# The norm of x taken behind PSUM, value columns first, and the first nine entries in written order

## The chip, the cores and the metric

The kernel runs on one NeuronCore of one Trainium2 chip. The metric is device time in microseconds (us) of one launch, a median over runs; lower is better. The clock of TensorE (PE in the rows) has two levels, 1.2 and 2.4 GHz. VectorE is DVE, ScalarE is ACT, GpSimd is POOL, and SyncE (SP) issues the DMAs.

## The reference

Two transformer blocks run on one sequence of 256 tokens with 1024 features. Only the beginning matters here: the root-mean-square norm of x and the projection of the first block.

```python
def rmsnorm(x, g):
    xf = x.astype(jnp.float32)
    y = xf * lax.rsqrt(jnp.mean(xf * xf, axis=-1, keepdims=True) + EPS)
    return (y * g.astype(jnp.float32)).astype(x.dtype)
...
        hn = rmsnorm(h, norm_mix_g[l])
        proj = hn @ w_in[l]
        fq, fk, fv, ff, gq, gf, gi, gg = jnp.split(proj, split_idx, axis=-1)
```

fq, fk, fv and the forget logits ff (8 columns) feed a causal attention, gq, gf, gi and gg a gated linear recurrence (HGRN). Everything is float32. The norm of a token is one factor per row of x, so it may be applied before the projection or to its result.

## The kernel before, in words

Every large product is made of three float32r matmuls: each operand is split into a high part, rounded to float32r, and the low rest, and `mm3` (L205 to L208) multiplies high by high, low by high, high by low. Weights come from HBM as granules of 1 MB (`Granule`, `feed`, three raw buffers `w`), one DMA each on SP's queue, issued as soon as a raw buffer is free. A granule is used in two halves. Each half is split by `split_next`: ACT casts it (tile `wh`, L142), DVE subtracts (tile `wl`, L143), into one of six pairs of split buffers.

The program is a list of entries (`prog`). An entry is one half of a granule, a unit of 24 matmuls of 256 columns or 12 of 512, with the pieces of other work that are hung behind it. `emit` walks the list: it writes the unit, then calls `pump`, which splits one further half, then the evacuation of PSUM (`evac`), then the pieces. In the kernel before `start` splits both halves of the first granule before any unit, so a unit's own half is always two calls of `pump` behind it. TensorE's order is the written one. For the other engines a scheduler sets the order from its own estimate of times; only `start` runs under a manual schedule (L737).

`start` loads the gain and x (L631, L633) and the first granule, warms TensorE with 12 matmuls of the identity (L642), squares x, takes the row factor with a power on POOL (L297), scales x (L651, L653), turns it with 16 transposes (L669) and splits the turned x into `xh` and `xl` (L328, L329). The gain is applied in that split.

Then come the projections of block one, in this order: gf (4 units, sigmoid), gq (4, silu), gg (4, silu), fv with ff (4), fq and fk (8), gi (4), and the keys of the memory attention (8). Hung behind them are `vectors` (turns small vectors, L693), `forget` (two activations with different tables, L930 and L931, and a scan), the nine levels of the recurrence, `m_load` and two `m_s` (load and norm of the memory rows: squares at L304, scaling at L315) and `load_later` with `difference` (four loads of lambda, L719, and a few instructions on `lamv`, L725 to L729, which only block two needs). PSUM tiles `mm` have two buffers, so the third unit pair needs the first one's evacuation.

Of the kernel before, what the change touches and what calls it, by code (L numbers as in the profile page):

```python
# [39 lines left out]
def two_blocks(ctx: ExitStack, tc: tile.TileContext, a: dict, out: bass.AP):  # L40
# [48 lines left out]
    def s_t():  # L89
        return psum.tile([P, 512], F32, tag="s", name=nm("s"), bufs=4)  # L90
# [26 lines left out]
    def feed():  # L117
        while at_dma[0] < len(stream) and at_split[0] >= 2 * (at_dma[0] - N_RAW + 1):
            g = stream[at_dma[0]]
            g.raw = wraw.tile([P, g.nk, g.ncol], F32, tag="w", name=nm("w"))  # L120
            src = g.src.rearrange("(k p) c -> p k c", p=P)
            if at_dma[0]:
                nc.sync.dma_start(g.raw, src)
            else:
                for c in (slice(0, P), slice(P, 2 * P)):
                    nc.sync.dma_start(g.raw[:, :, c], src[:, :, c])
            at_dma[0] += 1

    def split_next(pieces=None, low=V):
        g, i = stream[at_split[0] // 2], at_split[0] % 2  # L130
        if g.by_col:
            c = g.ncol // 2
            src, shape = g.raw[:, :, i * c:(i + 1) * c], [P, g.nk, c]
        else:
            k = g.nk // 2
            src, shape = g.raw[:, i * k:(i + 1) * k, :], [P, k, g.ncol]
        hi = wspl.tile(shape, F32R, tag="wh", name=nm("wh"))
        lo = wspl.tile(shape, F32R, tag="wl", name=nm("wl"))
        g.parts[i] = (hi, lo)
        at_split[0] += 1  # L140
        if pieces is None:
            S.copy(hi, src)  # L142
            low.tensor_tensor(lo, src, hi.bitcast(F32), op=ALU.subtract)  # L143
        else:
            k = g.nk // 2
            for p in (np.s_[:, 0:k, :], np.s_[:, k:, :]):
                def piece(p=p):
                    S.copy(hi[p], src[p])
                    G.tensor_tensor(lo[p], src[p], hi[p].bitcast(F32), op=ALU.subtract)
# [31 lines left out]
    def emit():  # L181

        for fn, pieces in prog:
            evac = fn() if fn is not None else None
            todo = later[:]
            later.clear()
            for f in todo:
                f()
            if fn is not None:
                pump()  # L190
            if evac is not None:
                evac()
            for f in pieces:
                f()
# [10 lines left out]
    def mm3(o, lh, ll, rh, rl, first, last):  # L205
        PE.matmul(o, lh, rh, start=first, stop=False)  # L206
        PE.matmul(o, lh, rl, start=False, stop=False)  # L207
        PE.matmul(o, ll, rh, start=False, stop=last)  # L208
# [109 lines left out]
    def xn_half(t):  # L318
        return R[4][:, t * D:(t + 1) * D]
# [306 lines left out]
    w_in = a["w_in"][0]  # L626

    def start():
        xin = a["x"][0].rearrange("(t p) d -> p t d", p=P)
        grow = R[5][0:8, 0:P]  # L630
        nc.sync.dma_start(grow, a["norm_mix_g"][0].rearrange("(k p) -> k p", p=P))  # L631
        for t in range(2):
            nc.sync.dma_start(h[:, t, :], xin[:, t, :])  # L633
        feed()
        V.memset(half, -0.5)
        V.memset(one, 1.0)
# [8 lines left out]
        o = [x.rearrange("p (k t) -> p k t", k=2) for x in (s_t(), s_t(), s_t(), s_t(), tp_t(), tp_t())]  # L645
        o = [o[k][:, 0, :] for k in range(6)] + [o[k][:, 1, :] for k in (2, 3)]

        def scale(t, n, r):
            x = xn_half(t)[:, HALVES[n]]
            if n > t:  # L650
                S.mul(x, h[:, t, HALVES[n]], r[:, 0:1])  # L651
            else:
                V.tensor_scalar(x, h[:, t, HALVES[n]], r[:, 0:1], None, op0=ALU.mult)  # L653

        ss = [sm_t(), sm_t()]
        for n in range(2):
            square(h[:, 0, HALVES[n]], ss[0][:, n:n + 1], (S, V)[n])
        r0 = rstd_row(ss[0])
        scale(0, 0, r0)
        for n in range(2):  # L660
            square(h[:, 1, HALVES[n]], ss[1][:, n:n + 1], (S, V)[n])
        scale(0, 1, r0)
        r1 = rstd_row(ss[1])
        for n in range(2):
            scale(1, n, r1)
        V.tensor_copy(g, go)
        for t in range(2):
            for k in range(8):
                PE.transpose(o[k][:, t * P:(t + 1) * P], xn_half(t)[:, k * P:(k + 1) * P], ident)  # L669
# [41 lines left out]

        def load_tables():
# [174 lines left out]
    def fv_units():  # L887
        gs_ = [Granule(w_in[kq * 512:(kq + 1) * 512, 1024:1544], 4, 520, False) for kq in range(2)]
        st = {}

        def unit(i):
            if i == 0:
                st["o"] = [(mm_t(), tp_t()) for _ in range(2)]
            w = part(gs_[i // 2], i % 2)
            for t in range(2):
                tok = slice(t * P, (t + 1) * P)
                for k in range(2):
                    for c in range(2):
                        cs = slice(c * 260, (c + 1) * 260)
                        mm3(st["o"][t][c][:, 0:260], r32(xh[:, 2 * i + k, tok]), r32(xl[:, 2 * i + k, tok]),  # L900
                            w[0][:, k, cs], w[1][:, k, cs], i == 0 and k == 0, i == 3 and k == 1)
            release()

            def ev():
                for t in range(2):
                    copy = V.tensor_copy if t else S.copy
                    o = st["o"][t]
                    ff.append(sm_t())
                    copy(fv[:, t, 0:260], o[0][:, 0:260])
                    copy(ff[t], o[1][:, 252:260])  # L910
                    copy(fv[:, t, 260:512], o[1][:, 0:252])
            return ev if i == 3 else None

        return [(lambda i=i: unit(i), gs_[i // 2] if i % 2 == 0 else None) for i in range(4)]
# [113 lines left out]
    u_ = []  # L1028
    for g in range(2):
        u_ += a_units(cols(w_in, 2056, g), XT, ev_gf(g))  # L1030
    for g in range(2):
        u_ += a_units(cols(w_in, 1544, g), XT, ev_silu(q_[:, g * 512:(g + 1) * 512]))
    u_ += b_units(w_in[:, 3080:3592], XT, lambda t, o: ev_silu(gs[:, t * 512:(t + 1) * 512])(0, o))
    u_ += fv_units()
    for g in range(2):
        u_ += a_units(cols(w_in, 0, g), XT, ev_to(R[2][:, g * 512:(g + 1) * 512], 0.125))
        u_ += a_units(cols(w_in, 512, g), XT, ev_to(R[2][:, 1024 + g * 512:1024 + (g + 1) * 512]))
    u_ += rows(w_in, 2568, 1, gi) + grid(xkw, 0, 4, R[5], None, ME)
    fox = Heads(fox_scores, fox_turn, fox_pv)
    run(u_, {  # L1040
        1: [lambda: start.vectors()], 2: [lambda: start.load_tables()], 6: [lambda: start.tables()],
        7: [lambda: start.load_later()], 9: [levels[0]], 11: [levels[1]],
        12: [m_load, levels[2], lambda: start.difference()], 13: [levels[3]], 14: [levels[4]], 15: [forget],
        16: [levels[5], m_s0], 17: [levels[6]], 18: [levels[7], m_s1, load_bias(0)], 19: [levels[8]],
        20: [load_bias(1, 2, 3)], 21: [fox.S(0)], 23: [fox.T(0), fox.S(1)], 25: [fox.V(0), m_t0],
        26: [fox.S(2), m_t1], 27: [fox.T(1)], 28: [fox.S(3), h_out(0)], 29: [fox.V(1), h_out(1)],
        30: [fox.T(2)], 31: [h_turn(0)], 32: [fox.V(2), fox.T(3)], 33: [h_turn(1)], 34: [fox.V(3)],
    })
# [338 lines left out]
    emit()  # L1387
# [49 lines left out]
```

## Time and profile before

| | |
|---|---|
| Median of 3 runs | 915.65 us (915.59 to 916.92) |
| The profiled execution's own time | 914.16 us |
| Its span, first to last instruction | 912.3 us |
| PE busy | 898.0 us (98%) |
| DVE busy | 588.4 us (64%) |
| ACT busy | 488.8 us (54%) |
| POOL busy | 130.0 us (14%) |
| HBM read | 160.34 MB, 177 GB/s over the span |

A timeline row reads: start and duration in us from the span's start, engine, source line, operation, out<-in tiles, partitions x elements, count, and in brackets the idle time before it with what ended it. Rows of equal instructions that follow each other are merged. PE's busy time counts overlapping matmuls, so the distance between the starts of two matmuls is the pace.

### The profile page before, as it was taken

Reading aid. Unit: us, or ns where it says so; the run is one execution under the profiler, and the core shown is the slowest. Engines: PE = TensorE matmul, PEld = TensorE weight load, DVE = VectorE, ACT = ScalarE, POOL = GpSimd, SP = SyncE. Lnnn points to the kernel's source line nnn. Section 1 sums busy time; section 2 is a strip of 40 time slices with the busy share of each in tenths; the row PEclk is TensorE's granted clock in tenths of the full one; section 3 lists DMA queues with packets and bytes.
Section 4 is the critical chain, followed back from the end, with each engine's and each line's share of the span. In section 5 each row is a group of like instructions: output and inputs, shape, how many; then the busy total and the mean of one; then the engine's idle time right before and its main releaser. Section 6 shows DMA issues by size and latency. Waiting matters only on the chain.

```text
span 912.3 us, 15217 instructions
## 1 busy us (share of the span) xinstructions
PE 898.0 (98%) x6213; PEld 823.9 (90%) x6213; DVE 588.4 (64%) x858; ACT 488.8 (54%) x743; POOL 130.0 (14%) x141
## 2 busy tenths in 40 slices
PE   8999999999999999999999999999999999999997
PEld 7999898898899999999898899999998789999995
DVE  5778775755575444555776455776756777766664
ACT  6745753555455444444654545667443676555552
POOL 3102220000002111111104000221211201101101
PEclk9999999999999999999999999999999999999999
DMA  8776544543555555555374555434555455555531
GB/s 271 256 253 186 185 155 164 198 153 114 167 193 192 195 190 193 189 185 185 131 250 135 183 179 185 139 131 133 200 185 185 161 185 183 188 201 193 166 135 47
DMA packets 117972, 162.39 MB, mean 178 GB/s; under 512 B 3647, under 2 KB 90509, under 8 KB 117901
## 3 DMA queue, kind: packets, MB, share of 16 engines
q1 hardware_dynamic: 117901, 161.41, 53.4%
q8 instruction: 49, 0.80, 0.3%
q14 instruction: 22, 0.18, 0.1%
HBM read 160.34 MB, written 1.06 MB: 177 GB/s over the span
## 4 chain that ended last, share of the span: by engine, by line
PE 90%; DVE 4%; ACT 2%; DMA 2%; POOL 1%; issue 1%; SPq 0%; DVEq 0%; POOLq 0%; ACTq 0%
PE mm L206 19%; PE mm L207 19%; PE mm L208 19%; PE s L208 8%; PE s L206 8%; PE s L207 8%; DMA w<-in_w_in_dram 2%; PE s L792 1%; POOL sm L297 1%; DVE wl L143 1%; PE tp L1068 1%; PE s L1060 1%; PE tp L337 1%; ACT wh L142 1%; PE s L1212 1%
## 5 line engine op out<-in xcount | busy, mean ns | idle before, releaser
L143 DVE TENSOR_TENSOR wl<-w,wh 128x1024 fp32r<-128x1024 f32 (+1 forms) x283 | 355.4, 1261 | 182.4 <-ACT wh L142 180.8
L142 ACT CAST wh<-w 128x1024 fp32r<-128x1024 f32 (+1 forms) x284 | 296.1, 1048 | 306.0 <-PE mm L207 190.2
L206 PE MATMUL mm<-xh,wh 128*128 128x256 f32 x1120 | 317.8, 284 | 0.0
L207 PE MATMUL mm<-xl,wh 128*128 128x256 f32 x1120 | 313.9, 280 | 0.3
L208 PE MATMUL mm<-xh,wl 128*128 128x256 f32 x1120 | 313.3, 280 | 0.0
L206 PEld LDWEIGHTS mm<-xh,wh 128*128 128x128 f32 x1120 | 211.3, 189 | 3.9 <-issue 2.3
L207 PEld LDWEIGHTS mm<-xl,wh 128*128 128x128 f32 x1120 | 211.2, 189 | 2.0 <-DVE xl L329 0.7
L208 PEld LDWEIGHTS mm<-xh,wl 128*128 128x128 f32 x1120 | 211.3, 189 | 0.0
L206 PE MATMUL s<-wh,mh 128*128 128x512 f32 x176 | 69.8, 396 | 0.0
L207 PE MATMUL s<-wl,mh 128*128 128x512 f32 x176 | 69.0, 392 | 0.0
L208 PE MATMUL s<-wh,ml 128*128 128x512 f32 x168 | 66.1, 393 | 0.0
L297 POOL TENSOR_TENSOR sm<-sm,half 128x1 f32<-128x1 f32 (+2 forms) x24 | 20.3, 847 | 234.2 <-DVE sm L310 221.7
L1103 POOL TENSOR_TENSOR r<-r 128x512 f32<-128x512 f32 x16 | 25.3, 1583 | 148.6 <-ACT r L1101 148.6
L206 PE MATMUL mm<-eh,wh 128*128 128x256 f32 x160 | 45.7, 286 | 0.0
L207 PE MATMUL mm<-el,wh 128*128 128x256 f32 x160 | 44.8, 280 | 0.0
L208 PE MATMUL mm<-eh,wl 128*128 128x256 f32 x160 | 44.7, 280 | 0.0
L208 PE MATMUL s<-wh,mh 128*128 128x512 f32 x112 | 44.1, 393 | 0.0
L1362 POOL TENSOR_TENSOR r<-r 128x512 f32<-128x512 f32 x11 | 21.4, 1946 | 148.0 <-DVE r L1350 124.2
L206 PE MATMUL s<-wh,ml 128*128 128x512 f32 x104 | 40.9, 394 | 0.0
L207 PE MATMUL s<-wl,ml 128*128 128x512 f32 x104 | 40.7, 392 | 0.0
L207 PEld LDWEIGHTS s<-wl,mh 128*128 128x128 f32 x176 | 33.1, 188 | 6.9
L206 PEld LDWEIGHTS s<-wh,mh 128*128 128x128 f32 x176 | 33.1, 188 | 6.7
(273 smaller groups left out, 1377.7 us busy)
## 6 DMA issues: line engine op xcount, KB each, us to landing
w<-in_w_in_dram SPq DMA_DIRECT2D x39, 1024.0 KB
w<-in_w_dram SPq DMA_DIRECT2D x32, 1024.0 KB
w<-in_w_up_dram SPq DMA_DIRECT2D x22, 1024.0 KB
w<-in_w_down_dram SPq DMA_DIRECT2D x11, 1024.0 KB
w<-in_w_xkv_dram SPq DMA_DIRECT2D x8, 1024.0 KB
w<-in_w_out_dram SPq DMA_DIRECT2D x8, 1024.0 KB
w<-in_w_xq_dram SPq DMA_DIRECT2D x4, 1024.0 KB
w<-in_w_xo_dram SPq DMA_DIRECT2D x4, 1024.0 KB
```

What stands on the lines that cost most here:

```text
L142: S.copy(hi, src)
L143: low.tensor_tensor(lo, src, hi.bitcast(F32), op=ALU.subtract)
L206: PE.matmul(o, lh, rh, start=first, stop=False)
L207: PE.matmul(o, lh, rl, start=False, stop=False)
L208: PE.matmul(o, ll, rh, start=False, stop=last)
L297: G.tensor_tensor(r[:, :n], v[:, :n], half.to_broadcast([P, n]), op=ALU.pow)
L337: PE.transpose(o[:, k * P:(k + 1) * P], xn[:, kk * P:(kk + 1) * P], ident)
L792: PE.matmul(o, k_[:, x], q2, start=True, stop=True)
L1060: PE.matmul(s[:, t, :], xq[:, j, t * P:(t + 1) * P], xkT[:, j, :], start=(c == 0), stop=(c == 1))
L1068: PE.matmul(o[:, c * T:(c + 1) * T], xv[:, m, cs], pt[:, m, :], start=(m == 0), stop=(m == 1))
L1103: G.tensor_tensor(tt, ra, ra, op=ALU.mult)
L1362: G.tensor_tensor(yv, yg, yv, op=ALU.mult)
```

## The change

- `start` turns x as it is, without its norm, in 16 transposes of h. The gain is still applied in the split of the turned x, now token half by token half. The row factors are made later (`factor`), kept as a column (`rt`) and, by one matmul (`row_factors`), as a row on all partitions (`rB`). They multiply each projection on its way out of PSUM: in `ev_gf` and `ev_token` on DVE ahead of the sigmoid or silu, elsewhere as the scale of the copy.
- The fv units come first, and x is split k by k as they need it.
- The first nine entries (`emit(9)`) get a chain of dependencies per engine, for ACT, DVE, POOL and SP, that keeps their instructions in written order (`in_order`). Instructions of later entries have no such chain. In these nine entries `pump` runs behind the evacuation instead of ahead of it.
- The pieces are hung at other entries, and the gain's load goes to ACT's queue.

```diff
     def do(*pieces):
         prog.append((None, list(pieces)))
 
+    @contextmanager
+    def in_order():
...
+            if i >= n and ins.engine in last:
+                tc.add_manual_dep(ins, last[ins.engine].name,
...
+    def emit(first=0):
...
+        for i, (fn, pieces) in enumerate(prog):
+            with (in_order() if i < first else nullcontext()):
+                evac = fn() if fn is not None else None
...
+                if fn is not None and i >= first:
+                    pump()
+                if evac is not None:
+                    evac()
+                if fn is not None and i < first:
+                    pump()
+                for f in pieces:
+                    f()
...
+    def split_x(i, t):
+        for k in (2 * i, 2 * i + 1):
+            split_to(XT, np.s_[:, k, t * P:(t + 1) * P], turned(t, k), start.g[:, k:k + 1])
+
+    def factor(t):
+        ss = sm_t()
+        for n in range(2):
+            square(h[:, t, HALVES[n]], ss[:, n:n + 1], (S, V)[n])
+        V.tensor_copy(rt[:, t:t + 1], rstd_row(ss)[:, 0:1])
...
-        for _ in range(12):
+        for _ in range(8):
             PE.matmul(o, ident, ident, start=True, stop=True)
...
+        pieces = []
+        for low in (V, G):
+            split_next(pieces, low)
+
+
         for t in range(2):
             for k in range(8):
-                PE.transpose(o[k][:, t * P:(t + 1) * P], xn_half(t)[:, k * P:(k + 1) * P], ident)
+                PE.transpose(turned(t, k), h[:, t, k * P:(k + 1) * P], ident)
+            split_x(0, t)
+            if t == 0:
+                for piece in pieces[0:2]:
+                    piece()
+            fv_part(0, t)
+        release()
+        split_x(1, 0)
+        pieces[2]()
+        split_x(1, 1)
+        pieces[3]()
...
     def ev_gf(g):
         def ev(i, o):
             s = slice(g * 512, (g + 1) * 512)
-            S.activation(f_[:, s], o, AF.Sigmoid)
+            V.tensor_tensor(f_[:, s].rearrange("p (b t) -> p b t", b=2), o.rearrange("p (b t) -> p b t", b=2), rB2,
+                            op=ALU.mult)
+            S.activation(f_[:, s], f_[:, s], AF.Sigmoid)
...
-    emit()
+    emit(9)
```

What the built program then holds, in three places.

DVE where the turned x is split (`s` are the turned tiles, `lamv` and `lam` the lambda vectors of `difference`, an entry beyond the ninth). Before, the lambda instructions stood in the third pair of granules:

```order
L143 TENSOR_TENSOR wl_563<-w_429,wh_562 128x1040
L725 TENSOR_TENSOR lamv<-lamv 128x128
L726 TENSOR_REDUCE lam<-lamv 128x2
L143 TENSOR_TENSOR wl_579<-w_429,wh_578 128x1040
L728 TENSOR_TENSOR lam<-lam 128x1
L729 TENSOR_SCALAR lam<-lam 128x1
L143 TENSOR_TENSOR wl_628<-w_492,wh_627 128x1040
```

Now:

```order
L352 SCALAR_TENSOR_TENSOR xl<-s_110,g_130,xh 128x128
L352 SCALAR_TENSOR_TENSOR xl<-s_111,g_130,xh 128x128
L770 TENSOR_TENSOR lamv<-lamv 128x128
L352 SCALAR_TENSOR_TENSOR xl<-s_110,g_130,xh 128x128
L352 SCALAR_TENSOR_TENSOR xl<-s_111,g_130,xh 128x128
L771 TENSOR_REDUCE lam<-lamv 128x2
L352 SCALAR_TENSOR_TENSOR xl<-s_108,g_130,xh 128x128
L352 SCALAR_TENSOR_TENSOR xl<-s_109,g_130,xh 128x128
L773 TENSOR_TENSOR lam<-lam 128x1
```

The lambda instructions moved into the split of x for the second unit.

ACT around the evacuations of gf and gq. Before (`r_87` is the sigmoid's and the silu's target, `mm` the PSUM tile):

```order
L142 CAST wh_252<-w_115 128x1024
L142 CAST wh_280<-w_115 128x1024
L142 CAST wh_331<-w_117 128x1024
L142 CAST wh_362<-w_117 128x1024
L753 ACT_TABLE_LOAD
L753 ACTIVATE r_87<-mm_227 128x512
L142 CAST wh_397<-w_200 128x1024
L142 CAST wh_425<-w_200 128x1024
```

Now (`wh_439` and `wh_484` are the two halves of the second gf granule, `wh_517` the first of gq, `P_446` the scratch of `forget`):

```order
L797 ACT_TABLE_LOAD
L797 ACTIVATE r_87<-r_87 128x512
L138 CAST wh_439<-w_147 128x1024
L988 ACT_TABLE_LOAD
L988 ACTIVATE P_446<-P_446 8x256
L989 ACT_TABLE_LOAD
L989 ACTIVATE P_446<-P_446,one 8x256
L138 CAST wh_484<-w_147 128x1024
L797 ACT_TABLE_LOAD
L797 ACTIVATE r_87<-r_87 128x512
L138 CAST wh_517<-w_319 128x1024
```

The cast of a half stands directly behind the evacuation of the unit that runs ahead of it, where before four casts stood ahead of the first sigmoid.

DVE at the first of these evacuations now (`r_92` holds the memory rows, `r_90` the row factors); before, the scaling of memory rows stood among the levels:

```order
L333 TENSOR_SCALAR sm_852<-sm_823 128x1
L338 SCALAR_TENSOR_TENSOR r_92<-r_92,sm_854,g_708 128x512
L795 TENSOR_TENSOR r_87<-mm_366,r_90 128x512
L338 SCALAR_TENSOR_TENSOR r_92<-r_92,sm_854,g_708 128x512
L333 TENSOR_SCALAR sm_949<-sm_920 128x1
L338 SCALAR_TENSOR_TENSOR r_92<-r_92,sm_951,g_708 128x512 x2
L139 TENSOR_TENSOR wl_440<-w_147,wh_439 128x1024
```

Three scalings of memory rows moved ahead of the low part `wl_440`, two of them with a power on POOL between.

## Rows read from the trace of the kernel before

**Rows 1.** The page's first part: busy time by engine.

```profile
PE 898.0 (98%) x6213; PEld 823.9 (90%) x6213; DVE 588.4 (64%) x858; ACT 488.8 (54%) x743; POOL 130.0 (14%) x141
```

**Rows 2.** Waits of PE, 0 to 160 us: total, times, longest, in us.

```profile
PE s L669 <- DVE r L653: 0.9, 1, 0.9
```

**Rows 3.** Timeline from the start, all engines.

```profile
1.34 5.49 PE L642 MATMUL mm<-ident 128*128 128x128 f32 x24 [1.34 <-POOL ident masks.py:199]
...
5.98 0.56 POOL L297 TENSOR_TENSOR sm<-sm,half 128x1 f32<-128x1 f32 x1 [4.69 <-DVE sm L310]
...
7.12 0.66 PE L669 MATMUL s<-ident,r 128*128 128x128 f32 x4
...
10.73 1.57 ACT L328 ACTIVATE xh<-s,g 128x256 fp32r<-128x256 f32 x4 [1.55 <-DVE g L666]
...
11.24 1.66 DVE L329 SCALAR_TENSOR_TENSOR xl<-s,g,xh 128x256 fp32r<-128x256 f32 x4 [0.60 <-ACT xh L328]
...
14.49 0.19 PEld L207 LDWEIGHTS mm<-xl,wh 128*128 128x128 f32 x1 [0.33 <-DVE xl L329]
```

**Rows 4.** Chain of waits, 33 to 42 us: start, length, what.

```profile
35.00 0.12 PE mm L206
35.12 0.13 PE mm L207
35.27 1.06 ACT wh L142
36.33 0.51 ACT r L767
36.88 0.50 PE mm L206
```

**Rows 5.** Waits of SP, 0 to 60 us.

```profile
SPq L713 <- DMA w<-in_w_in_dram: 2.8, 1, 2.8
```

**Rows 6.** Timeline of SP, the table behind two granules and the lambda loads.

```profile
15.86 0.36 SPq L713 DMA_DIRECT2D lvlf<-in_c_lvl_dram  x1
...
33.58 1.00 SPq L719 DMA_DIRECT2D lamv<-in_lambda_k_dram  x2
```

**Rows 7.** Timeline of DVE, 40 to 43 us.

```profile
40.67 0.29 DVE L725 TENSOR_TENSOR lamv<-lamv 128x128 f32<-128x128 f32 x1 [3.42 <-DMA lamv<-in_lambda_k_dram]
```

**Rows 8.** Windows: busy us by engine, granted clock, DMA share, GB/s.

```profile
36.00:37.00 1.00, 0.86 (x5) 0.39 (x4) 1.00 (x2) 0.98 (x3) 0.00 (x0) 1.00 1.03 383
...
38.00:39.00 1.00, 1.00 (x6) 0.83 (x5) 0.00 (x0) 0.13 (x1) 0.00 (x0) 1.00 0.26 64
```

**Rows 9.** Groups by form: busy us, mean ns of one, idle before.

```profile
L143 DVE TENSOR_TENSOR wl<-w,wh 128x1024 fp32r<-128x1024 f32 x279 | 350.4, 1262 | 182.4 <-ACT wh L142 180.8
...
L315 DVE SCALAR_TENSOR_TENSOR r<-r,sm,g 128x512 f32<-128x512 f32 x8 | 5.8, 743 | 2.3 <-POOL sm L297 2.3
...
L1176 DVE TENSOR_TENSOR r<-mm,r 128x512 f32<-128x512 f32 x8 | 5.5, 689 | 3.1 <-PE mm L208 3.0
...
L142 ACT CAST wh<-w 128x1024 fp32r<-128x1024 f32 x280 | 292.0, 1048 | 305.7 <-PE mm L207 189.9 <-PE s L208 58.5 <-PE mm L208 27.1
...
L304 ACT ACTIVATE junk<-r 128x512 bf16<-128x512 f32 x8 | 4.9, 620 | 0.0
...
L753 ACT ACTIVATE r<-mm 128x512 f32<-128x512 f32 x2 | 1.2, 601 | 0.0
```

**Rows 10.** Timelines of ACT and DVE where `forget` ran.

```profile
70.26 1.28 ACT L930 ACT_TABLE_LOAD   x1
...
73.89 0.51 ACT L931 ACTIVATE P<-P,one 8x256 f32<-8x256 f32 x1
...
76.56 0.67 DVE L936 TENSOR_TENSOR_SCAN P<-P 8x256 f32<-8x256 f32 x1
```

**Rows 11.** Windows at the kernel's end, columns as in rows 8.

```profile
906.00:908.00 2.00, 0.00 (x0) 0.00 (x0) 1.44 (x4) 0.97 (x3) 0.56 (x2) 0.97 0.00 0
908.00:910.00 2.00, 0.00 (x0) 0.00 (x0) 1.12 (x2) 0.00 (x0) 0.84 (x1) 0.50 0.40 134
```

More of the change, by code (lines that the diff above doesn't have):

```diff
@@ L1 @@
-from contextlib import ExitStack
+from contextlib import ExitStack, contextmanager, nullcontext
 import numpy as np
@@ L121, in feed @@
             src = g.src.rearrange("(k p) c -> p k c", p=P)
[L122 to L126, printed above, removed]
+            nc.sync.dma_start(g.raw, src)
             at_dma[0] += 1
@@ L148, in piece @@
                     S.copy(hi[p], src[p])
[L149 removed]
+                    low.tensor_tensor(lo[p], src[p], hi[p].bitcast(F32), op=ALU.subtract)
                 pieces.append(piece)
@@ L202, in then, with mm3 @@
         later.append(go)
-    def mm3(o, lh, ll, rh, rl, first, last):
+    def mm3(o, lh, ll, rh, rl, first, last, rl_last=False):
         PE.matmul(o, lh, rh, start=first, stop=False)
-        PE.matmul(o, lh, rl, start=False, stop=False)
-        PE.matmul(o, ll, rh, start=False, stop=last)
+        if rl_last:
+            PE.matmul(o, ll, rh, start=False, stop=False)
+        PE.matmul(o, lh, rl, start=False, stop=last and rl_last)
+        if not rl_last:
+            PE.matmul(o, ll, rh, start=False, stop=last)
     def a_units(src, xt, evac, nk=8):
@@ L710, in tables, with row_factors @@
             G.memset(attn, 0.0)
+        def row_factors():
+            ones, diag = R[4][:, 0:P], R[4][:, P:3 * P]
+            G.memset(ones, 1.0)
+            for t in range(2):
+                V.tensor_scalar(diag[:, t * P:(t + 1) * P], ident, rt[:, t:t + 1], None, op0=ALU.mult)
+            o = s_t()[:, 0:T]
+            PE.matmul(o, ones, diag, start=True, stop=True)
+            V.tensor_copy(rB, o)
         def load_tables():
@@ L885, in two_blocks @@
     ff = []
[L887 to L894, printed above, removed]
-            for t in range(2):
[L896 to L914, printed above, removed]
@@ new lines, in two_blocks, with fv_part @@
+    fv_g = [stream[0], Granule(w_in[512:D, 1024:1544], 4, 520, False)]
+    fv_o = []
+    def fv_part(i, t):
+        if len(fv_o) == t:
+            fv_o.append((mm_t(), tp_t()))
+        w = part(fv_g[i // 2], i % 2)
+        tok = slice(t * P, (t + 1) * P)
+        for k in range(2):
+            for c in range(2):
+                cs = slice(c * 260, (c + 1) * 260)
+                mm3(fv_o[t][c][:, 0:260], r32(xh[:, 2 * i + k, tok]), r32(xl[:, 2 * i + k, tok]),
+                    w[0][:, k, cs], w[1][:, k, cs], i == 0 and k == 0, i == 3 and k == 1, True)
@@ new lines, in fv_unit, with ev @@
+    def fv_unit(i):
+        for t in range(2):
+            fv_part(i, t)
+        release()
+        if i < 3:
+            for t in range(2):
+                split_x(i + 1, t)
+            factor(i - 1)
+        def ev():
+            for t in range(2):
+                o, r = fv_o[t], rt[:, t:t + 1]
+                ff.append(sm_t())
+                for dst, src in ((fv[:, t, 0:260], o[0][:, 0:260]), (ff[t], o[1][:, 252:260]),
+                                 (fv[:, t, 260:512], o[1][:, 0:252])):
+                    if t:
+                        V.tensor_scalar(dst, src, r, None, op0=ALU.mult)
+                    else:
+                        S.mul(dst, src, r)
+        return ev if i == 3 else None
@@ L1027, in two_blocks @@
     m_load, m_s0, m_s1, m_t0, m_t1 = mem_rows("mem", "norm_mem_g", R[5], s_t)
-    u_ = []
+    u_ = [(lambda i=i: fv_unit(i), fv_g[1] if i == 2 else None) for i in range(1, 4)]
     for g in range(2):
@@ L1035, in two_blocks @@
     for g in range(2):
-        u_ += a_units(cols(w_in, 0, g), XT, ev_to(R[2][:, g * 512:(g + 1) * 512], 0.125))
-        u_ += a_units(cols(w_in, 512, g), XT, ev_to(R[2][:, 1024 + g * 512:1024 + (g + 1) * 512]))
-    u_ += rows(w_in, 2568, 1, gi) + grid(xkw, 0, 4, R[5], None, ME)
-    fox = Heads(fox_scores, fox_turn, fox_pv)
[L1040 to L1048, printed above, removed]
+        u_ += a_units(cols(w_in, 0, g), XT, ev_token(R[2][:, g * 512:(g + 1) * 512], 0.125))
@@ L1049, in two_blocks @@
+    run(u_, {i - 1: x for i, x in at.items()})
     fill_xv = rows(xkw, D, 2, xv, ME)
```

118 lines of the change are left out of this document (63 added, 55 removed).

## The prediction

> **What bounds the kernel now.** I read the page's busy times first: TensorE is busy for 898.0 of 912.3 us [rows 1]. Then the waits of TensorE up to 160 us, where the whole change lies: the longest that the view names is 0.9 us, in the start [rows 2]. Then the chain of waits, which shows one more: the matmul at 35.12 ends at 35.25 and the next starts at 36.88, 1.6 us later, behind a cast and an evacuation on ACT [rows 4]. Last the timeline, for durations. So the time is TensorE's matmuls at their pace, 0.12 us for 256 columns [rows 4], plus what TensorE stands still. Only standstill can be won or lost, and I count that. In the start the last gap ends at 14.49 [rows 3] and 19 matmuls of 256 columns lie ahead of it; 14.49 - 19 x 0.12 = 12.2, as if the matmuls had begun there without a gap. Standstill before: 12.2 + 1.6 = 13.8 us.
>
> What the change offers is the start. What it costs is read from the order: in the first nine entries the cast of the next half stands behind the evacuation of the present unit, on an engine that works in that order. TensorE needs the half at once, so each evacuation becomes a gap. I follow the clock from the start.
>
> **Step 1: x without its norm, fv first.** Warming takes 8 instead of 12 matmuls at 5.49 / 12 = 0.46 [rows 3], and ends at 1.34 + 3.7 = 5.0. Eight transposes of a token half take 8 x 0.15 = 1.2 (0.66 for four with the last one's tail [rows 3]). High and low parts of 128 columns I put at 0.3 each: 256 columns took 1.57 / 4 = 0.39 and 1.66 / 4 = 0.42 [rows 3], part of it fixed. With the low parts of the second half on POOL, the slower engine, TensorE would have three of fv's eight token parts done near 15.4 (estimated).
>
> It can't go on, because DVE's next low part of x stands behind L770 on `lamv`. The lambda loads are on SP behind x (1.05 MB), both fv granules (2.13) and the first gf granule (1.05), 4.2 MB. Before, the first 4.2 MB on the same queue had landed at 15.86, when the eighth DMA behind was let go [rows 5, 6]. SP starts x 0.46 us sooner now, and its rows are longer; I take 14.8. Before, the lambda loads were issued until 34.58 behind one granule and DVE got them at 40.67 [rows 6, 7], after windows in which the granule's 383 GB/s fell to 64 [rows 8]: some 3.5 us after the granule's data. So they land at about 18.0. Bounds: 15.4, landing with the gf granule, and 19.5, each of the four costing as much as the slowest stretch shows.
>
> From 18.0 DVE has, ahead of the low part of the third fv half: two lambda instructions (0.29 each [rows 7]), six low parts of x (1.8), two small lambda ones with a round trip to ACT (0.5), the square of a row (0.7, as 512 columns elsewhere [rows 9]), sum, POOL's power at 0.56 [rows 3] and copy (1.1), then 1.26 [rows 9]: it ends at 23.7. TensorE has two matmuls of that unit out already, then 22 x 0.12 = 2.65, until 26.4. The fourth half repeats it: four parts of x, with ACT between them, square, power, copy, low part, to 28.0, and 2.65 more: fv ends at 30.65. If the lambda loads didn't hold DVE, the same chain would go on at about 12 and end at 24.6. Fv's 96 matmuls take 11.5, so standstill is 19.1 against 12.2: **+6.9**.
>
> **Step 2: fv's evacuation.** The first gf half is cast behind the evacuation. Token half 0 is copied by ACT before fv ends, token half 1 by DVE after it, 1.1 us; only then the low part, 1.26; then two scaled identities (0.5) and the row factors' matmul (0.45, estimated), which stands ahead of the gf unit. TensorE starts gf at 34.1: **+3.45**.
>
> **Step 3: first gf evacuation.** Two units of 2.85 and the two small transposes of `vectors` end at 40.05, `forget`'s transposes at 40.35. ACT has, ahead of the sigmoid, the exponential of `vectors` and four squares of memory rows (0.7 each with their reads [rows 9]) that were drawn in from later entries, then a table load of 1.28 [rows 10]: the sigmoid starts at 42.7, ends at 43.3, the cast at 44.3 [rows 9]. DVE has the product with the row factors (0.69) and three scalings of memory rows (0.74 each) with a power between [rows 9], and ends the low part at 46.7. TensorE's third matmul waits for that: 46.75 - 40.35 less two matmuls = **+6.2**. The unit ends at 49.4.
>
> **Step 4: second gf half.** Its cast stands behind `forget` on ACT: DVE's four instructions on 8 rows until 47.9, load 1.28, exponential 0.4, load 1.28, logarithm 0.51 [rows 10], cast 1.05: 52.4. DVE's scan (0.67 [rows 10]) comes first, then the low part, to 54.05. 54.05 - 49.4 less 0.24 = **+4.4**. The unit ends at 56.7.
>
> **Step 5: second gf evacuation.** Product 0.69, sigmoid 0.6, cast 1.05, low part 1.26 [rows 9] and hand-overs: 60.45. **+3.5**.
>
> **Step 6: gg.** From entry ten the scheduler may run ahead, but DMA is behind: a raw buffer came free only as late as the splits. The second gg granule can be issued at 65.4, lands near 70.8, and DVE's product for the second gq pair stands behind its low part, at 77.2. TensorE needs that PSUM tile for gg's second token half and waits 4.2 in all, where the kernel before waited 1.6 [rows 4]: **+2.6**. Bounds: -1.6 if no gap opens here at all, +4.2 if the old one opens besides.
>
> **No cost.** DVE's products at the evacuations of gf, gq, fq and fk are eight of 0.69 [rows 9], 5.5 us. Behind gg they lie beside matmuls, on an engine busy for 64% of the span [rows 1]; if that cover goes, each of the last four costs its 0.69. The eight transposes per token half are as many as before, and the gain's load on ACT's queue only frees SP.
>
> Sum: 6.9 + 3.45 + 6.2 + 4.4 + 3.5 + 2.6 = **27 us**. The profiled execution took 914.16, so 941.2; the median of the runs is 1.5 higher, so I predict 942.7. A measurement of this kernel can tell 0.2% (1.8 us) from no change.
>
> **A rule beside the rows.** At the kernel's end, in stretches without a matmul, the granted clock goes to 0.97 and then to 0.50 [rows 11]: 1.2 GHz, where the stretches with matmuls show 1.00 [rows 8]. The Trainium skill, in "TensorE: Matmul & The Clock Gate", section "Why this matters for your kernels", warns against gaps between bursts for the same reason; by it several gaps here would be followed by matmuls at half pace, and the time would be the clock rival's below. A half-pace unit after step 3 costs nothing, since the next waits for step 4 anyway.
>
> **Rivals.**
> 1. *The clock falls in more gaps.* A unit at half pace loses 24 x 0.12 = 2.9 us. Exposed are the units behind steps 2, 4, 5 and 6, and about 1 us in step 1: up to +12; with two of them about 948. For it: gaps of 3.5 to 6 us. Against: single matmuls in them. Chance 0.27.
> 2. *No lambda wait.* If the loads pass the granules and land by 12, step 1 ends at 24.6 instead of 30.65: 936.7. For it: the loads are small. Against: 6.1 us behind a single granule [rows 6, 7]. Chance 0.1.
> 3. *Faster.* If the casts ran ahead of the evacuations, no gap of steps 2 to 5 would open. First matmul at 5.0 + 0.2 + 1.2 + two parts (0.6) and a cast: near 7.6, against 11.2, where DVE's first low part starts now [rows 3]: 3.6 won, and the 1.6 of the chain [rows 4] too: 910.4. It decides where ACT's cast `wh_439` starts: before the first sigmoid's input is there, or after. The printed order excludes it unless the engine reorders. Chance 0.03.
> 4. *The order isn't what limits*, gaps are filled and the start gives back what they cost: within 0.2%. Chance 0.02.
>
> The forecast case, 936 to 948, has 0.58; the chances of slower add up to 0.95. **The range** goes from 932 (lambda at 15.4 and no gap in step 6: 27 - 2.6 - 4.2 leaves 20, and 4 us less if my small estimates are a fifth too long) to 955 (all of the clock's 12).
>
> **What would show it.** Right: DVE stands at L770 until about 18; the first gf matmul near 34; casts at L138 right behind the sigmoids at L797; some 17 us of idle TensorE between 30 and 63; the pace after 90 us as before. Wrong: lambda in before 12, gf running before 30, or gaps under 1 us at the sigmoids. If the granted clock is under 1.00 over whole units, the clock rival is at work.

## The result, and the profile after

| | before | changed |
|---|---|---|
| Median | 915.62 us, 4 runs (914.29 to 916.92) | 954.22 us, 4 runs (953.18 to 954.84) |
| Span of the profiled execution | 912.3 us | 952.2 us |
| Mean granted clock | 0.998 | 0.985 |

The change makes the kernel slower by a factor of 1.042 (95% interval 1.0402 to 1.0439), 38.6 us. The forecast was 27 us slower, 942.7; the range held the time.

The page's busy times, to set beside [rows 1], and its row of the granted clock, 24 us to a digit:

```profile
PE 919.0 (97%) x6207; PEld 839.3 (88%) x6207; DVE 595.5 (63%) x876; ACT 486.0 (51%) x746; POOL 130.4 (14%) x140
...
PEclk8979999999999999999999999999999999999999
```

TensorE has six matmul records fewer and is busy 21 us longer; the span is 40 us longer. So only half of the loss is idle time: the rest is in the matmuls themselves. To see where, I split both spans at the first matmul on `eh`, the same instruction in both programs. Ahead of it lies the same work but for the warming and the row factors (821 matmul records before, 815 after); behind it both have 5,392. Timeline of TensorE, kernel before, then changed:

```profile
114.78 0.37 PE L206 MATMUL mm<-eh,wh 128*128 128x256 f32 x1
```

```profile
144.81 0.38 PE L226 MATMUL mm<-eh,wh 128*128 128x256 f32 x1
```

Ahead of it the change costs 144.81 - 114.78 = 30.0 us. Behind it 952.2 - 144.81 = 807.4 against 912.3 - 114.78 = 797.5, another 9.9, where no matmul has changed.

**The first part.** Waits of TensorE, 0 to 145 us (total, times, longest), to set beside [rows 2]:

```profile
PE mm L226 <- ACT wh L138: 7.5, 4, 3.4
PE mm L228 <- DVE xl L352: 3.8, 1, 3.8
PE mm L231 <- DVE wl L139: 3.7, 3, 1.7
PE s L754 <- DVE r L752: 2.4, 1, 2.4
PE mm L229 <- DVE wl L139: 2.1, 2, 1.0
```

These lines sum to 19.5 us of waiting, 13.3 of it for a cast (L138) or a low part (L139) of the next half. The longest of them in the timeline of TensorE, in the order of the prediction's steps 1 to 5:

```profile
19.36 0.59 PE L228 MATMUL mm<-wh,xl 128*128 128x260 f32 x1 [3.77 <-DVE xl L352]
...
33.56 1.19 PE L754 MATMUL s<-r 128*128 128x256 f32 x2 [2.36 <-DVE r L752]
...
45.17 0.39 PE L226 MATMUL mm<-xh,wh 128*128 128x256 f32 x1 [3.39 <-ACT wh L138]
47.40 0.58 PE L231 MATMUL mm<-xh,wl 128*128 128x256 f32 x1 [1.72 <-DVE wl L139]
53.07 0.39 PE L226 MATMUL mm<-xh,wh 128*128 128x256 f32 x1 [1.50 <-ACT wh L138]
54.79 0.58 PE L231 MATMUL mm<-xh,wl 128*128 128x256 f32 x1 [1.22 <-DVE wl L139]
62.24 0.39 PE L226 MATMUL mm<-xh,wh 128*128 128x256 f32 x1 [2.38 <-ACT wh L138]
63.50 0.39 PE L231 MATMUL mm<-xh,wl 128*128 128x256 f32 x1 [0.76 <-DVE wl L139]
```

What stands behind two of them, on DVE and ACT (to set beside [rows 7, 10]): the lambda product that waits 6.85 us, and sigmoid, cast, `forget`, cast in that order.

```profile
18.75 0.29 DVE L770 TENSOR_TENSOR lamv<-lamv 128x128 f32<-128x128 f32 x1 [6.85 <-DMA st<-in_hgrn_lb_logits_dram]
```

The view puts this wait down to another small load of the same queue. The product reads `lamv` alone, the last of whose four loads lands at 18.63 by the trace's semaphore updates, and e3 below settles it.

```profile
43.56 0.63 ACT L797 ACTIVATE r<-r 128x512 f32<-128x512 f32 x1
44.09 1.03 ACT L138 CAST wh<-w 128x1024 fp32r<-128x1024 f32 x1
48.56 1.28 ACT L988 ACT_TABLE_LOAD   x1 [3.44 <-issue]
...
51.99 1.03 ACT L138 CAST wh<-w 128x1024 fp32r<-128x1024 f32 x1
```

And the clock. Windows (columns as in [rows 8]):

```profile
55.00:60.00 5.00, 4.86 (x22) 4.56 (x22) 0.10 (x1) 0.00 (x0) 0.00 (x0) 0.50 0.71 214
...
70.00:74.00 4.00, 4.00 (x36) 4.00 (x35) 3.40 (x7) 2.90 (x4) 1.00 (x2) 1.00 0.75 258
```

From 55 to 60 us, behind the waits listed from 45.17 to 54.79, nearly a whole unit runs at a granted clock of 0.50, 1.2 GHz: 22 matmuls in 5 us, 0.21 us each. At 70 it is 1.00 again. The low stretches by the distance of matmul starts are 19.4 to 23, 34.2 to 36.5, 47.4 to 50.3, 54.8 to 59.9 and 63.5 to 67.3.

**The second part.** Groups by form, from 150 us on in the kernel before and from 180 on in the changed one (busy us, mean ns of one):

```profile
L207 PE MATMUL mm<-xl,wh 128*128 128x256 f32 x992 | 277.5, 280 | 0.0
...
L386 PE MATMUL tp<-ident,P 128*128 128x128 f32 x32 | 4.8, 272 | 0.0
```

```profile
L229 PE MATMUL mm<-xl,wh 128*128 128x256 f32 x992 | 280.3, 283 | 0.0
...
L409 PE MATMUL tp<-ident,P 128*128 128x128 f32 x32 | 4.8, 272 | 0.0
```

Nearly every form that reads a split weight, `wh` or `wl`, is 1 to 4 ns slower; the small transposes are not. The mean distance from the start of such a matmul to the next of the same size, over all of them behind the split point, says the same: 118.4 ns before and 120.5 after at 256 columns (3,577 and 3,578 pairs), 233.5 and 235.8 at 512 (1,227 pairs each), some 2.2 ns more in both. 3,577 x 2.2 ns + 1,227 x 2.2 ns = 10.6 us, against 9.9 lost. The granted clock reads 1.00 in both. What differs is the address: the new constant tile `rt` (two columns) takes 32 bytes a partition, and the pools behind the constants move by that. The built programs have the split weights at addresses 154816 + n x 4160 before and 154848 + n x 4160 after: multiples of 64 before, 32 off after. A second difference is that `s` now takes the first four PSUM banks and `mm` the next two, since the start asks for `s` first.

### The profile page after: what moved, and what is told of

It is laid out like the page before. It is cut to its first block, busy times and chain, and to the rows that moved or that the text cites. A ratio compares the mean times of both kernels' runs of the same rounds, so it can differ in the third digit from the quotient of the medians.

```text
span 952.2 us, 15244 instructions
## 1 busy us (share of the span) xinstructions
PE 919.0 (97%) x6207; PEld 839.3 (88%) x6207; DVE 595.5 (63%) x876; ACT 486.0 (51%) x746; POOL 130.4 (14%) x140
## 4 chain that ended last, share of the span: by engine, by line
PE 86%; DVE 5%; DMA 3%; ACT 3%; issue 2%; POOL 1%; SPq 1%; DVEq 0%; POOLq 0%; ACTq 0%
PE mm L226 18%; PE mm L229 18%; PE mm L231 18%; PE s L231 8%; PE s L226 7%; PE s L229 7%; DMA w<-in_w_in_dram 2%; DVE wl L139 1%; POOL sm L320 1%; PE s L843 1%; ACT wh L138 1%; DMA r<-negF 1%; PE tp L1129 1%; PE s L1121 1%; PE tp L360 1%
## 5 line engine op out<-in xcount | busy, mean ns | idle before, releaser
L139 DVE TENSOR_TENSOR wl<-w,wh 128x1024 fp32r<-128x1024 f32 (+1 forms) x283 | 354.8, 1259 | 191.9 <-ACT wh L138 190.3
L138 ACT CAST wh<-w 128x1024 fp32r<-128x1024 f32 (+1 forms) x284 | 296.0, 1047 | 318.9 <-PE mm L229 208.2
L226 PE MATMUL mm<-xh,wh 128*128 128x256 f32 x1120 | 322.9, 288 | 7.3 <-ACT wh L138 7.3
L231 PE MATMUL mm<-xh,wl 128*128 128x256 f32 x1120 | 319.1, 285 | 3.7 <-DVE wl L139 3.7
L229 PE MATMUL mm<-xl,wh 128*128 128x256 f32 x1120 | 318.9, 285 | 0.0
L226 PEld LDWEIGHTS mm<-xh,wh 128*128 128x128 f32 x1120 | 214.0, 191 | 12.0 <-ACT wh L138 8.1
L231 PEld LDWEIGHTS mm<-xh,wl 128*128 128x128 f32 x1120 | 213.9, 191 | 4.3 <-DVE wl L139 4.3
L229 PEld LDWEIGHTS mm<-xl,wh 128*128 128x128 f32 x1120 | 214.2, 191 | 1.4
L1423 POOL TENSOR_TENSOR r<-r 128x512 f32<-128x512 f32 x11 | 21.8, 1985 | 150.5 <-DVE r L1411 116.1
L229 PE MATMUL mm<-wl,xh 128*128 128x512 f32 (+1 forms) x96 | 36.9, 385 | 3.0 <-DVE wl L139 2.1
L226 PE MATMUL mm<-wh,xh 128*128 128x512 f32 (+1 forms) x96 | 38.1, 396 | 1.7 <-ACT wh L144 0.9
```

Of the source, the lines that this page charges most:

```text
L229: PE.matmul(o, lh, rl, start=False, stop=last and rl_last)
L1423: G.tensor_tensor(yv, yg, yv, op=ALU.mult)
```

## The experiments

The kernel before ran beside each batch; its median was 913.5 (e1 to e4), 913.6 (e5 to e8), 915.3 (e9 to e11) and 913.8 us (e12). The ratio to it is the figure to compare; the changed kernel's is 1.042. "First" is the start of the first matmul on `eh`, "rest" the span less that.

| run | median us | ratio, 95% | first | rest |
|---|---|---|---|---|
| before | 915.62 | 1 | 114.8 | 797.5 |
| changed | 954.22 | 1.042 (1.0402 to 1.0439) | 144.8 | 807.4 |
| e1_pad64 | 943.69 | 1.0326 (1.0309 to 1.0343) | 145.7 | 797.0 |
| e2_before_shift32 | 924.11 | 1.0119 (1.0098 to 1.0140) | 116.0 | 806.0 |
| e3_lambda_late | 947.05 | 1.0359 (1.0339 to 1.0378) | 141.5 | 807.0 |
| e4_pump_first | 946.16 | 1.0352 (1.0336 to 1.0368) | 137.6 | 807.2 |
| e5_three | 928.03 | 1.0159 (1.0144 to 1.0174) | 129.8 | 796.7 |
| e6_forget_late | 929.20 | 1.0172 (1.0155 to 1.0189) | 130.4 | 796.6 |
| e7_lead2 | 923.61 | 1.0110 (1.0095 to 1.0126) | 125.2 | 796.7 |
| e8_fill | 941.23 | 1.0303 (1.0288 to 1.0318) | 143.2 | 796.7 |
| e9_split_shift | 926.36 | 1.0121 (1.0099 to 1.0142) | 118.5 | 806.5 |
| e10_best_f5 | 917.14 | 1.0023 (1.0014 to 1.0032) | 118.7 | 796.6 |
| e11_best_f10 | 918.29 | 1.0037 (1.0022 to 1.0051) | 118.0 | 796.8 |
| e12_best_f12 | 915.10 | 1.0016 (1.0006 to 1.0026) | 116.1 | 796.4 |

The rest takes one of two values, 796.4 to 797.5 or 806.0 to 807.4, whatever is done to the first part.

**The address (e1, e2, e9).** Expected of e1:

> The changed kernel with the new tile rt made 64 bytes wide a partition instead of 8 (which take 32): the weight tiles, raw and split, start on a multiple of 64 bytes again, as before the change; no instruction moves. Theory (the 32-byte shift slows every matmul that reads a split weight): the steady pace of the 256-column matmuls goes back from 0.119 to 0.117 us, of the 512-column ones from 0.234 to 0.231, and the time falls by 8 to 11 us, to about 945. Rival (the pace changed for another reason, such as the PSUM banks, which the change also deals out in another order): the pace stays at 0.119 and the time at 954 within 1.5 us.

```diff
-    rt = const.tile([P, 2], F32, name="rt")
+    rt = const.tile([P, 16], F32, name="rt")
```

Expected of e2:

> The kernel before with one constant tile (g8) widened from 8 to 16 columns, which moves the weight tiles behind it by 32 bytes a partition; every engine keeps its instructions and its order, and the PSUM banks stay. Theory (the shift): 8 to 11 us slower than before, about 925, spread over the whole span with no new wait. Rival (not the shift): 915.6 within 1.5 us.

```diff
-        g = const.tile([P, 8], F32, name="g8")
+        g = const.tile([P, 16], F32, name="g8")[:, 0:8]
```

Expected of e9:

> The kernel before with an unused 32-byte pool ahead of the pool of split weights and another behind it: wh and wl alone start 32 bytes off a multiple of 64, the raw weights ahead of them and all tiles behind them keep their place modulo 64; no instruction and no order changes. Theory (it is TensorE's reads of the shifted wh and wl that take longer): as e2, 8 to 11 us over the kernel before, with a pace of 0.119 us for 256 columns. Rival (the raw tiles that DMA writes and ACT and DVE read, or the tiles behind, P, PT and junk, cost it): 913.6 within 2 us and a pace of 0.117.

```diff
+    pad1 = ctx.enter_context(tc.tile_pool(name="pad1", bufs=1))
     wspl = ctx.enter_context(tc.tile_pool(name="wspl", bufs=N_SPLIT))
+    pad2 = ctx.enter_context(tc.tile_pool(name="pad2", bufs=1))
...
+    for pad in (pad1, pad2):
+        pad.tile([P, 8], F32, name="pad")
```

The theory holds each time. With `rt` at 64 bytes the rest is back at 797.0, though the PSUM banks stay as the change deals them, so these cost nothing. The kernel before with 32 bytes more loses 1.19%, and 1.21% with the split weights alone shifted. Groups by form behind 160 us, e2 and then e9:

```profile
L207 PE MATMUL mm<-xl,wh 128*128 128x256 f32 x992 | 279.6, 282 | 0.0
```

```profile
L209 PE MATMUL mm<-xl,wh 128*128 128x256 f32 x992 | 279.7, 282 | 0.0
```

The mean distance at 256 columns, taken as above, is 120.2 ns in e2 and 120.3 in e9 (3,577 pairs each), 118.4 in e1; at 512 columns it is 236.2, 236.3 and 233.5. So it is TensorE's reads of `wh` and `wl`; why 32 bytes cost them something isn't shown. DVE and ACT don't mind: low part and cast took 1259 and 1047 ns in the changed kernel, 1262 and 1048 before [rows 9]. The Trainium skill, in "SBUF — State Buffer", section "Specifications (TRN2)", gives 16-byte cachelines and a penalty for each cross to a new line, and nothing on what an operand's start address costs. A shift of two whole lines changes no crossing, so nothing there leads one to expect what these runs show: 1.9 to 2.2 ns more at 256 columns.

**The lambda loads (e3).**

> The changed kernel with the order of ACT, DVE, POOL and SP fixed for the first 20 entries instead of 9 (pump still ahead of the evacuation from entry 9 on): the lambda loads and their five DVE and ACT instructions, and the mem rows' loads and squares, stand at their own entries and no longer among the first granules. Theory (step 1 on record): the wait of 6.85 us on DVE at 11.9 to 18.75 goes, the value columns end near 25 instead of 31.1, and the time falls by 5 to 8 us, to 946 to 949. Rival (the w_in loads that stand behind arrive no sooner, or the half-speed stretches move along): less than 2 us.

```diff
-            with (in_order() if i < first else nullcontext()):
+            with (in_order() if i < max(first, last) else nullcontext()):
...
-    emit(9)
+    emit(9, 20)
```

The wait on DVE is gone, and the last matmul of fv starts at 24.80 instead of 30.92; the prediction had 24.6 for this case. Timeline of TensorE:

```profile
24.80 0.28 PE L229 MATMUL tp<-wl,xh 128*128 128x260 f32 x1
27.45 0.77 PE L754 MATMUL s<-r 128*128 128x256 f32 x1 [2.37 <-DVE r L752]
```

The time falls by 0.6% of the kernel before, 5.6 us: about the 6 of step 1. But the edit also takes the squares and scalings of the memory rows away from the first gf evacuation, so what is the lambda loads' alone is the end of fv, 6.1 us sooner. The profiled execution took 950.33 us, the others 945.95 to 947.57, so its "first" in the table is high.

**The split behind the evacuation (e4).**

> The changed kernel with the split of the next half written ahead of the evacuation in the ordered entries too, as everywhere else; the order stays fixed for nine entries. Theory (steps 3 and 5 on record: the hi and lo of the next half stand behind the evacuation on ACT and DVE, and TensorE waits for them): the waits of 3.4, 1.7, 2.4 and 0.8 us of TensorE near 45, 47, 62 and 63.5 go or shrink to under 1 us each, and the time falls by 6 to 10 us, to 944 to 948. Rival (the granule lands too late for an earlier split, so that the cast blocks the evacuation instead): within 2 us of 954.

```diff
-                if fn is not None and i >= first:
+                if fn is not None:
                     pump()
                 if evac is not None:
                     evac()
-                if fn is not None and i < first:
-                    pump()
```

The gain is 0.7%, 6.2 us, inside the expectation. But one wait takes the place of several: TensorE now waits 5.13 us for the half that stands behind `forget`.

```profile
48.95 0.58 PE L224 MATMUL mm<-xh,wh 128*128 128x256 f32 x1 [5.13 <-ACT wh L138]
```

On ACT that is the cast behind `forget`'s two table loads:

```profile
46.16 1.28 ACT L987 ACT_TABLE_LOAD   x1
47.45 0.51 ACT L987 ACTIVATE P<-P,one 8x256 f32<-8x256 f32 x1
47.87 1.98 ACT L138 CAST wh<-w 128x1024 fp32r<-128x1024 f32 x2
```

**The three together, and `forget` moved (e5, e6).**

> The changed kernel with three edits at once: the tile rt of 64 bytes, the order fixed for 20 entries (lambda and mem work at their own entries), and the split of the next half ahead of the evacuation. Theory (three separate causes): the gains add, 8.6 to 10.5 for the alignment, 5.6 to 7.2 for lambda, 6.2 to 8.1 for the split, so 20 to 26 us less than 954, that is 928 to 934. Rival (lambda's wait and the late split cover one another, since both leave the same half late): 14 to 18 us less, 936 to 940.

The ratios gain 0.94 + 0.61 + 0.68 = 2.2% one by one and 2.6% together: within the intervals the gains add, so none of the causes is hidden behind another.

> The kernel of e5 with forget moved from the fifth entry to the fifteenth and the first bias loads from the eighth to the eighteenth, so that forget's two ACT table loads and its DVE steps leave the four entries of f and q. Theory (step 4 on record, 4.4 us, of which part is already gone with the earlier split): 2 to 5 us less than e5. Rival (with the split ahead of it forget holds nobody that TensorE waits for): within 1.5 us of e5.

```diff
-        2: [lambda: start.load_tables()], 3: [lambda: start.row_factors()], 4: [lambda: start.vectors()], 5: [forget],
-        8: [load_bias(0)], 7: [lambda: start.tables()], 11: [lambda: start.load_later()],
+        2: [lambda: start.load_tables()], 3: [lambda: start.row_factors()], 4: [lambda: start.vectors()],
+        7: [lambda: start.tables()], 11: [lambda: start.load_later()],
...
+        13: [levels[0], m_load], 14: [levels[1]], 15: [levels[2], lambda: start.difference(), forget], 16: [levels[3], m_s0],
+        17: [levels[4]], 18: [levels[5], m_s1, load_bias(0)], 19: [levels[6]], 20: [levels[7]], 21: [levels[8], fox.S(0)],
```

No gain: 1.0172 against 1.0159. The wait that `forget` causes only moves, from 39.65 in e5 to 78.86 in e6. Timelines of TensorE, e5 and e6:

```profile
39.65 0.39 PE L224 MATMUL mm<-xh,wh 128*128 128x256 f32 x1 [3.41 <-ACT wh L138]
```

```profile
78.86 0.58 PE L224 MATMUL mm<-xh,wh 128*128 128x256 f32 x1 [3.54 <-ACT wh L138]
```

So it isn't the place. In the kernel before the same table loads [rows 10] kept nobody waiting, with two halves split ahead.

**The second half ahead (e7).**

> The kernel of e6 with one more half split in the second entry, so that TensorE has two halves ahead of it, as in the kernel before, instead of one. Theory (what is left of the gaps is the lead: each split of 1.2 us on ACT and 1 us on DVE behind an evacuation, a table load or the vectors is waited for when only one half is ahead): the waits of 2 to 3 us at the units of f go, TensorE keeps 2.4 GHz, and the time falls by 5 to 10 us below e6, to 915 to 923. Rival (the granules land too late for an earlier split): within 2 us of e6.

```diff
                 if fn is not None:
                     pump()
+                    if i == 1:
+                        pump()
```

0.6% better, 5.7 us, the smaller end of what was expected, and no wait on a cast or low part of an f, q or gate half is left over 0.6 us. What is left is one wait of 2.1 us for the row factors' diagonals and one of 3.8 among the levels, where `forget` now stands on DVE.

```profile
PE s L843 <- DVE r L853: 3.8, 1, 3.8
PE s L754 <- DVE r L752: 2.1, 1, 2.1
PE mm L226 <- DVE r L814: 1.4, 1, 1.4
```

**The clock by itself (e8).**

> The kernel of e1 (rt of 64 bytes) with 35 products of the identity by itself, 128 columns each, about 0.23 us apiece, put where TensorE waits: 8 ahead of the row factors' product, 12, 4, 8 and 3 ahead of the units of f's second granule and of q's first. Their output is overwritten; ACT, DVE, POOL and SP keep their instructions and order. Theory (the rival 1 on record, as a part of the loss: TensorE falls to half pace behind these gaps, 127 matmuls in e1's trace, 12 us): the matmuls behind the filled gaps keep 0.117 us, and the time falls by 5 to 10 us below e1's 943.7, to 934 to 939. Rival (the pace behind a gap hangs on the gap's cause, not on TensorE being idle; or the slow pace is hidden by the casts that bound these units anyway): within 2 us of e1, or slower by the fillers that don't fit, up to 4 us.

```diff
+    fills = {"rf": 8, 3: 12, 4: 4, 5: 8, 6: 3}
...
+        for _ in range(fills.get(key, 0)):
+            PE.matmul(o, ident, ident, start=True, stop=True)
```

Windows of e1 and of e8:

```profile
34.00:45.00 11.00, 8.21 (x54) 7.88 (x54) 5.60 (x17) 4.37 (x11) 2.08 (x3) 0.84 0.47 160
45.00:52.00 7.00, 4.37 (x18) 4.08 (x19) 4.64 (x10) 3.53 (x5) 1.92 (x3) 0.58 0.22 76
```

```profile
34.00:45.00 11.00, 9.78 (x80) 9.43 (x80) 6.38 (x19) 5.51 (x12) 2.39 (x4) 1.00 0.48 163
45.00:52.00 7.00, 3.86 (x31) 3.57 (x30) 4.18 (x9) 3.98 (x5) 1.51 (x2) 1.00 0.24 76
```

With the gaps filled the granted clock is 1.00 in both stretches. But the ratio falls from 1.0326 to 1.0303 only, 0.23% or 2.1 us, and the two intervals overlap: short of the 5 to 10 expected, and not to be told from the rival's bound of 2. A unit that ends sooner waits longer for the cast that isn't there. At 52.50 TensorE waits 1.92 us in e8 for the same cast L138 that cost 0.78 in e1, and the next stretch, 52 to 60, is at 0.57 again. From 18.6 to 28.9, where nothing was filled, the clock stays at 0.50. So the run tells what filling these gaps gives, not what the low clock costs in all.

**A version without the gaps (e10, e11, e12).** The three edits of e5, the second half ahead, and the diagonals two entries ahead of their product; they differ in the entries of `forget` and of the first bias loads, and e12 in the order of one evacuation.

> The three edits of e5, one more half split in the second entry as in e7, and the diagonals of the row factors made two entries ahead of their product instead of behind the value evacuation; forget stays at the fifth entry. Theory (what is left in e7 is the wait of 2.1 us for the diagonals with the 2.4 us at half pace behind it, and the 3.8 us that forget costs DVE among the levels): 912 to 918. Rival (with forget among f and q its two table loads on ACT are waited for even with two halves ahead): 919 to 924.

```diff
+        def row_diag():
+            G.memset(ones, 1.0)
+            for t in range(2):
+                V.tensor_scalar(diag[:, t * P:(t + 1) * P], ident, rt[:, t:t + 1], None, op0=ALU.mult)
...
-        2: [lambda: start.load_tables()], 3: [lambda: start.row_factors()], 4: [lambda: start.vectors()], 5: [forget],
+        2: [lambda: start.row_diag(), lambda: start.load_tables()], 3: [lambda: start.row_factors()], 4: [lambda: start.vectors()], 5: [forget],
```

> As e10, with forget at the tenth entry and the first bias loads at the fourteenth: behind q, ahead of the levels, where DVE and ACT have the least to do. Theory: no wait over 1.5 us is left for TensorE between 8 and 120 us, and the time is 911 to 916, level with the kernel before or a little under. Rival (forget only moves a wait of the gate values' evacuation): 917 to 922.

```diff
+        7: [lambda: start.tables()], 10: [forget], 11: [lambda: start.load_later()],
+        13: [levels[0], m_load], 14: [levels[1], load_bias(0)], 15: [levels[2], lambda: start.difference()], 16: [levels[3], m_s0],
```

> As e11, with forget one entry into the gate values (twelfth, the bias loads at the sixteenth), and in the eleventh entry alone the evacuation ahead of the next split. Theory (e11's waits of 3.1 and 1.1 us for DVE's product of q are forget's two steps and one split that stand ahead of it; nothing waits for an evacuation while the gate values run): both go, 3 to 4 us less than e11, 913 to 915, level with the kernel before or up to 2 us under it. Rival (the levels start later behind forget, or the gate values' halves are split too late): within 1.5 us of e11, 917 to 919.

```diff
-                if fn is not None:
+                if fn is not None and i != 11:
                     pump()
...
                 if evac is not None:
                     evac()
+                if i == 11:
+                    pump()
...
+        12: [forget], 13: [levels[0], m_load], 14: [levels[1]], 15: [levels[2], lambda: start.difference()], 16: [levels[3], m_s0, load_bias(0)],
```

e10 fits its theory. e11 misses: `forget` stands ahead of DVE's product of q, which the first gate unit needs, 4.2 us in all. e12 removes that, but gains 0.21%, 1.9 us, where 3 to 4 were expected: 1.0016 (1.0006 to 1.0026), level with the kernel before by the 0.2% that counts here and not under it. Its waits of TensorE, 0 to 120 us:

```profile
PE mm L694 <- POOL ident masks.py:199: 1.3, 1, 1.3
PE mm L228 <- DVE r L819: 1.1, 1, 1.1
PE mm L231 <- DVE wl L139: 1.1, 2, 0.6
PE s L848 <- DVE r L869: 1.0, 1, 1.0
PE mm L228 <- ACT wh L144: 0.9, 1, 0.9
PE mm L231 <- POOL wl L145: 0.8, 2, 0.5
```

The waits of the kernel before, 0 to 115 us, beside [rows 2]:

```profile
PE mm L642 <- POOL ident masks.py:199: 1.3, 1, 1.3
...
PE tp L669 <- DVE r L653: 0.8, 1, 0.8
PE s L924 <- DVE sm L910: 0.5, 1, 0.5
```

In e12 none is over 1.3 us, yet these lines sum to 6.2, against 1.3 + 0.9 + 0.8 + 0.5 = 3.5 before. The first matmul on a split weight starts at 6.84 in e12 and at 11.26 before, 4.4 us sooner; the 97th, behind the 96 of fv, at 23.18 and 23.94, 0.8 sooner; the first on `eh` at 116.1 and 114.8, later. So most of what an earlier first matmul wins goes within fv, which follows the cast of x and of its weights so closely. No version here beats the kernel before.

## Why the prediction was right or wrong

| step | predicted | trace |
|---|---|---|
| 1: DVE at the lambda product | until 18.0 | 18.75 |
| 1: end of fv | 30.65 | 31.0 |
| 2: f starts | 34.1 | 34.20 |
| 3: its third matmul after the first evacuation | 46.75 | 47.40 |
| 4: the same behind `forget` | 54.05 | 54.79 |
| 5: the same in q | 60.45 | 63.50 |
| 6: wait of TensorE at gg | 4.2 us at 77.2 | none |
| first matmul on `eh` | +27 | +30.0 |
| from there on | +0 | +9.9 |

Steps 1 to 4 hold to 0.75 us, and e3 (step 1) and e4 (steps 3 and 5) remove most of what they name. That a late lambda load holds fv, that the cast behind the evacuation makes each evacuation a gap, and that `forget` does it once more, is shown. For step 4 the reason was incomplete: e6 shows that moving `forget` gains nothing while one half is ahead, and e7 that with two no cast behind it is waited for; the lead of one half is what exposes it.

One reading of the prediction is wrong. In [rows 4] the chain leaves TensorE at 35.25 for ACT and comes back at 36.88, and the prediction took that for 1.6 us of standstill. A chain shows one path, not all that an engine does. Timeline of TensorE in the kernel before:

```profile
35.19 0.40 PE L206 MATMUL mm<-wh,xh 128*128 128x512 f32 x1
...
36.35 0.39 PE L208 MATMUL mm<-wh,xl 128*128 128x512 f32 x1
36.88 0.50 PE L206 MATMUL mm<-wh,xh 128*128 128x512 f32 x1
```

Six matmuls of 512 columns start from 35.19 to 36.35, and by their pace of 0.23 the next is only 0.3 us late. So the standstill before is 12.5 us and not 13.8, step 6 as forecast costs 3.9 and not 2.6, and the sum is 28.3, which gives 944.0. Rival 3 comes to 911.7. The longest wait of TensorE in the view of [rows 2] is 1.3 us, ahead of the warming, and not 0.9; it lies within the 12.2 and changes nothing.

Steps 5 and 6 are off in opposite directions, by the clock. The unit behind step 4 ran at half pace from 54.8 to 59.9 instead of 2.65 us, so step 5 came 3 us late, and q began at half pace as well. The sum had set the clock aside as rival 1, with a chance of 0.27. The wait of step 6 was then spent ahead of it: DVE's second product of q ended at 76.52 + 0.69 = 77.2, as forecast, but TensorE reached gg only at 76.32 and its second token half at 76.32 + 6 x 0.234 = 77.7. So there the kernel is 0.5 us behind the forecast's times, some 28.8 behind the kernel before by the sum put right. Rival 1 moved the waits rather than added to them, and e8, where the clock came back and little was won, agrees. The Trainium skill's warning of gaps between bursts ("TensorE: Matmul & The Clock Gate", section "Why this matters for your kernels") holds for the clock, which is at 0.50 behind the gaps and 1.00 where e8 fills them; filling them gave back 2.1 us, not clear of noise. The other 1.2 us up to the split point are argued, not shown: the slower pace over 67 us (about 0.9), and a wait of 1.0 for `P` that the kernel before hasn't.

What failed is the sentence "the pace after 90 us as before", and with it "Only standstill can be won or lost". They put at nothing a tile of eight bytes a partition. That term, 9.9 us, is most of the miss of 38.6 - 27 = 11.6. That the range held the time, by 0.8 us, is luck: its top stood for 12 us of the clock, and what filled it was a term that the prediction didn't have. The trace of before couldn't show it; the addresses of the built program could have shown that all weights move, not what that costs.

Rival 2 came out as priced where e3 made its condition true: fv ends at 24.8 without the lambda wait. Rival 3 did not: with the casts ahead (e7, e10 to e12) the gaps of its steps go, but neither 910.4 nor 911.7 was reached, since fv gives back most of what the earlier first matmul wins.

## What to carry to other kernels

When a change adds a tile, look at the addresses of every tile that TensorE reads: 32 bytes ahead of the weights cost 1.2% of this kernel, with no wait of TensorE to show for it and the granted clock at 1.00, so split both spans at a common instruction and compare the pace behind it. An order fixed by hand needs as many operands prepared ahead as its longest side job takes: with one half ahead evacuations and table loads became gaps, with two no cast or low part of these halves was waited for over 0.6 us (e7). A fixed order binds only what stands in it: work written later, and not in it, is drawn ahead, and its slow load then holds the engine. And a jump to another engine in a chain of waits isn't yet standstill: look at the engine's own timeline first.

## What the runs showed of the hardware

- Matmuls whose stationary or moving operand starts 32 bytes off a multiple of 64 take longer: by 1.9 to 2.2 ns at 256 columns, where the weight is stationary (118.4 ns before; 120.5, 120.2 and 120.3 in the changed kernel, e2 and e9), and by 2.2 to 2.7 ns at 512, where it moves (233.5; 235.8, 236.2 and 236.3). Shifting the split weights alone does it (e9). The small transposes that read the `P` tiles, shifted too in the changed kernel, kept their 272 ns. Other offsets weren't tried.
- Handing `mm` and `s` other PSUM banks changed nothing (e1, rest 797.0 against 797.5).
- Filling gaps with products that nobody uses kept the granted clock at 1.00 from 34 to 52 us, where it was 0.84 and 0.58, and gave 2.1 us, not clear of noise (e8 against e1).
